# Keys and values built beside the last projection chunk; scores and retention products in array groups of their own

## The chip, the cores and the metric

One core of one Trainium2 chip runs the whole step as one launch. The time is device time in microseconds, the median of the runs shown below.

## The reference, cut to what matters

The program is one step of a decoder layer with a prompt of 1024 tokens and 8 decode sequences of 4 tokens each, on a past of 1024 tokens in pages.

```python
z = rms_norm(x, norm_mix) @ w_in               # q, three K/V pairs, retention q/k/v, gate columns
# attention group: 8 heads of 64, 2 K/V heads; three branches, gated sum
o_cmp = softmax(q kc) vc                       # 63 compressed blocks
o_sel = softmax(q k[selected blocks]) v        # here 16 blocks of 64 keys; decode leaves one of 17 out
o_win = softmax(q k[last 512]) v
# retention group: 4 heads, chunks of 128 tokens, state of 64 x 128 per head
s = (q k^T) * dec ; o = s v + (q state) * cross
state = g^128 * state + (k * w)^T v
h = x + [nsa ; retention] @ w_out
y = h + (silu(conv3(u W_u)) * (u W_v)) W_d     # u = rms_norm(h)
```

Everything is float32. Outputs are y, the new K/V rows, the window buffers, the retention states and the convolution states.

## The kernel before, in words

The program is written with a planner: pools hand out tiles, each instruction gets a place in a priority order (the order of the text, moved forward by a `high_priority` offset), and the planner fixes the order on each engine, the DMA issues of SyncE among them. At run time each engine works through its own list strictly; a DMA that waits for a buffer holds those queued behind it.

**Products.** A float32 product is two TensorE instructions. Large products use a high and a low part (`split`, lines 120 to 122: ScalarE copies the high part, VectorE or GpSimd subtracts) and add three products of the parts.

**Projections.** Nine token tiles (eight of 128 prompt tokens, the ninth 32 decode tokens) stand split in `XT[0..8]` (line 140). Six chunks of columns follow each other: `run(c, f, ...)` (line 925) takes chunk c through all tiles, in rising or falling order. Chunks 0 and 1 give the K/V rows, chunks 2 and 3 the retention, chunk 4 the queries, chunk 5 the retention gates (`ret_gate`, line 291, order 8 down to 0). Between tiles `run` advances a side generator by a number of steps: `compress_phase` in chunks 0 to 3, `decode_phase` in chunks 4 (2.5 steps a tile from the fourth on) and 5 (1 step a tile).

**Retention** (line 315). For each chunk and head `ob[h]` is the product of the decayed scores `at` with the values (128 rows, line 353) and, from the second chunk, of the queries `qc` with the state (64 rows, upper or lower half of the partitions by the head, line 355), added in the same place of PSUM. The banks alternate with the head. Line 341 makes the scores (64 rows), line 359 the new state (128 rows into 64 output partitions, upper or lower).

**Decode** (line 618). For each of four pairs B of sequences: `window_branch` and the steps of `compressed`, then `selected_branch`. `scores` (line 682) multiplies a tile of keys by `QB`: its columns 0 to 31 hold the queries of the first sequence, 96 to 127 those of the second, the rest zeros; each of the two products uses 64 columns, so that together they fill all 64 output rows of `XB`, the second added to the first. There is a `yield`, the end of a step, behind each product of keys. Keys come by page loads (`load_page`, line 451) of 128 KB into `GA[0]` and `GA[1]`; the window branch uses `GA[0]`, and pages of the selected branch are loaded there when it is done (line 809). Pages and windows pass through one SyncE queue.

**Keys and values.** `build(i)` (line 1259) loads 256 KB of finished K/V rows of a token tile from the output, splits the values into `VS` (ScalarE and GpSimd), transposes the keys on TensorE, and splits them into `KS` (ScalarE and VectorE). `KS` and `VS` lie in a pool of their own (line 992). The staging tile `STG` and the tile `FIN`, into which the masks are loaded first (line 1253), lie in the place of the first projection's tiles (`p1`, released in line 976). Builds 0 to 3 stand in front of the attention, 4 to 7 are the first four steps of `rest()`.

**Attention** (line 1103). For each token tile in the order 3, 2, 7, 6, 1, 0, 5, 4, for two K/V heads and two branches (selected with all earlier keys; window with the compressed keys): `softmax` (line 1032) makes the scores of four heads, `values_of` (line 1079) transposes the probabilities in blocks of 128 keys, splits them, and multiplies them by `VS`, or, for the last block of a window branch, which has 64 compressed keys, by `VC` (64 rows, lines 1092 and 1093). Each piece yields a cost; `beside(gen, ratio, cost)` (line 1238) advances the attention by ratio x cost for each step of another generator: first `rest()` (the builds and what is left of decode, 1.32), then the splitting of the output weights into `WO` (1.44 x 2.0), then the output projections of pairs of tiles (1.63, 18 steps each). The last output projection runs when the attention has ended, and `ffn_early` (line 1405) beside it.

**FFN.** Its seven operand tiles `X[1..7]` and later the tiles `h` lie in `p3h` (1, 2, 3), and in the places of `WO` (6, 7, 5, 4); four tiles of split weights lie in the place of `MIX`.

## Time and profile before

| what | value |
|---|---|
| median of 3 runs | 1564.74 us (1562.82 to 1569.26) |
| profiled execution | 1569.05 us |
| its span (first to last instruction) | 1567.3 us |
| TensorE busy | 1504.3 us, 96% |
| VectorE / ScalarE / GpSimd busy | 66% / 46% / 43% |
| mean granted TensorE clock | 0.98 |

The page gives one execution. The span is what its engines show; the execution's own time is 1.75 us longer. A busy share is a mean over stages that differ, so the rows further down are cut by stage. Starts are in us from the start of the span. The granted clock is given as a share of 2.4 GHz. Ends of TensorE instructions are modelled and overlap; the distance between starts tells how long one holds the engine.

### The profile page before, as it was taken

The page shows a single profiled execution, that of the slowest core. Times are in us where ns is not written, and L with a number is a line of the kernel's source. Part 1 is how long each engine was busy: PE and PEld are TensorE (multiplying, and loading weights), DVE is VectorE, ACT ScalarE, POOL GpSimd, SP SyncE. Part 2 cuts the span into 40 slices and gives each one's busy share as a digit, 9 for nine tenths or more (in the row PEclk, how much of TensorE's full clock was granted, in tenths as well). Part 3 has the DMA queues.
Part 4 walks back from the last instruction along what each step waited for, and adds up shares of the span by engine and source line. Part 5 has one row for each costly group of instructions (what it writes and reads, how often), then busy time and mean ns, then how long its engine had stood idle before and what let it go on. Part 6 is the DMA issues. An engine that isn't in the chain of part 4 may idle for free.

```text
span 1567.3 us, 28652 instructions
## 1 busy us (share of the span) xinstructions
PE 1504.3 (96%) x10338; PEld 1344.1 (86%) x10338; DVE 1038.6 (66%) x2023; ACT 717.2 (46%) x1564; POOL 679.5 (43%) x945
## 2 busy tenths in 40 slices
PE   7999999999899997999999899999999999999999
PEld 5898877766566665798988899999999999999999
DVE  7876523364388788766566987778878877644631
ACT  6454323233577667755555443333333334544431
POOL 3553211262366547656544143333333334444542
PEclk9999999999899999999999999999999999999999
DMA  8452300231412211001013224555554534887662
GB/s 269 147 153 68 87 11 27 58 124 57 161 60 68 84 41 54 28 15 45 28 29 95 73 89 144 163 172 173 168 171 164 169 135 148 287 258 214 208 197 66
DMA packets 126274, 184.43 MB, mean 118 GB/s; under 512 B 20388, under 2 KB 84772, under 8 KB 126132
## 3 DMA queue, kind: packets, MB, share of 16 engines
q1 hardware_dynamic: 124644, 177.97, 35.8%
q0 software_dynamic: 1488, 4.63, 0.9%
q8 instruction: 81, 1.33, 0.3%
q14 instruction: 61, 0.50, 0.1%
HBM read 132.73 MB, written 49.82 MB: 116 GB/s over the span
## 4 chain that ended last, share of the span: by engine, by line
PE 81%; DVE 8%; ACT 4%; issue 3%; DMA 3%; SPq 1%; POOL 0%; DVEq 0%; ACTq 0%; POOLq 0%
PE PS L459 49%; PE PS L230 5%; PE PS L233 5%; PE PS L232 5%; PE PS L1088 3%; PE PS L1204 2%; PE PS L1203 2%; PE PS L1205 2%; DVE live L1053 1%; PE PS L683 1%; DVE pt L122 1%; PE PS L353 1%; PE PS L355 1%; ACT pt L121 1%; ACT pwin L1054 1%
## 5 line engine op out<-in xcount | busy, mean ns | idle before, releaser
L459 PE MATMUL PS<-x,wop 128*128 128x264 f32 x3696 | 455.7, 286 | 9.0 <-ACT x L121 3.7
L459 PEld LDWEIGHTS PS<-x,wop 128*128 128x128 f32 x3696 | 453.6, 189 | 10.8 <-ACT x L121 4.1
L459 PE MATMUL PS<-h,wop 128*128 128x264 f32 x1848 | 225.7, 284 | 0.0
L459 PEld LDWEIGHTS PS<-h,wop 128*128 128x128 f32 x1848 | 225.5, 188 | 0.0
L122 POOL TENSOR_TENSOR wop<-st,wop 128x512 fp32r<-128x512 f32 (+1 forms) x105 | 139.3, 1333 | 177.3 <-ACT wop L121 173.7
L121 ACT ACTIVATE wop<-st 128x512 fp32r<-128x512 f32 x150 | 90.5, 608 | 205.6 <-PE PS L459 113.2
L230 PE MATMUL PS<-wh,xt 128*128 128x512 f32 (+1 forms) x432 | 168.9, 393 | 8.0 <-ACT xt L121 7.8
L233 PE MATMUL PS<-wh,xt 128*128 128x512 f32 (+1 forms) x384 | 148.5, 387 | 2.6 <-DVE xt L122 2.6
L232 PE MATMUL PS<-wl,xt 128*128 128x512 f32 (+1 forms) x384 | 148.5, 387 | 0.0
L122 DVE TENSOR_TENSOR pt<-PS,pt 128x512 fp32r<-128x512 f32 (+1 forms) x148 | 100.0, 684 | 40.7 <-ACT pt L121 24.8
L122 POOL TENSOR_TENSOR wop<-rawf,wop 128x512 fp32r<-128x512 f32 x42 | 70.7, 1684 | 119.8 <-ACT wop L121 119.8
L121 ACT ACTIVATE pt<-PS 128x512 fp32r<-128x512 f32 (+1 forms) x148 | 86.3, 596 | 57.9 <-PE PS L1088 29.2
L1053 DVE TENSOR_REDUCE live<-PS 128x1 f32<-128x640 f32 (+7 forms) x128 | 88.0, 701 | 32.7 <-PE PS L459 31.3
L230 PEld LDWEIGHTS PS<-wh,xt 128*128 128x128 f32 x432 | 83.8, 195 | 29.3 <-ACT xt L121 8.5
L459 PE MATMUL PS<-ks,qt 128*128 128x320 f32 (+5 forms) x400 | 102.2, 350 | 5.6 <-ACT psel L1054 4.1
L459 PE MATMUL PS<-pt,vs 128*128 128x512 f32 x264 | 103.1, 444 | 4.2 <-ACT pt L121 1.8
L233 PEld LDWEIGHTS PS<-wh,xt 128*128 128x128 f32 x384 | 74.6, 194 | 16.8 <-DVE xt L122 3.5
L232 PEld LDWEIGHTS PS<-wl,xt 128*128 128x128 f32 x384 | 74.6, 194 | 15.0 <-issue 2.6
L1077 POOL TENSOR_TENSOR pwin<-pwin,live 128x64 f32<-128x64 f32 (+5 forms) x128 | 80.2, 651 | 2.2
L1203 PE MATMUL PS<-mix,wo 128*128 128x256 f32 (+1 forms) x256 | 74.8, 293 | 2.3 <-ACT mix L121 2.3
L1072 POOL TENSOR_TENSOR live<-live 128x1 f32<-128x1 f32 (+1 forms) x128 | 24.7, 199 | 119.2 <-DVE live L1071 98.8
L459 PEld LDWEIGHTS PS<-ks,qt 128*128 128x128 f32 x400 | 64.8, 197 | 13.4 <-ACT psel L1054 5.6
(400 smaller groups left out, 2999.1 us busy)
## 6 DMA issues: line engine op xcount, KB each, us to landing
rawf<-in_w_ffn_in SPq DMA_DIRECT2D x30, 512.0 KB, 3.3
rawf<-scr_x SPq DMA_DIRECT2D x51, 264.0 KB, 3.7
scr_x<-rbig SPq DMA_DIRECT2D x44, 264.0 KB, 2.6
ws<-in_w_ffn_out SPq DMA_DIRECT2D x64, 176.0 KB, 3.0
scr_s<-ws SPq DMA_DIRECT2D x64, 176.0 KB, 2.4
scr_x<-qbig SPq DMA_DIRECT2D x33, 264.0 KB, 2.1
raw<-in_w_in SPq DMA_DIRECT2D x17, 512.0 KB, 3.6
ga<-in_cache_sel SPq DMA_DIRECT2D x64, 128.0 KB, 2.0
```

The costliest lines, as they stand in the source:

```text
L121: a = S.activation(h, src, AF.Copy)
L122: return a.ins, (eng or V).tensor_tensor(l, src, b32(h), ALU.subtract).ins
L230: T.matmul(ps, xh(i, kk), wh[:, k], start=first, stop=False)
L232: T.matmul(ps, xh(i, kk), wl[:, k], start=False, stop=False)
L233: T.matmul(ps, xl(i, kk), wh[:, k], start=False, stop=end)
L459: T.matmul(o, a, b, start=start, stop=stop, skip_group_check=True)
L1053: V.tensor_reduce(nm[:, r:r + 1], src, AX.XY, ALU.max, negate=True)
L1077: G.tensor_tensor(a, a, f.to_broadcast([128, a.shape[1]]), ALU.mult)
L1088: T.transpose(tb[:, r * 128:(r + 1) * 128], pp[r][:, c:c + n], ident)
L1203: T.matmul(o, wh, MIX[:, 0, k, 0:n], start=k == 0, stop=False)
L1204: T.matmul(o, wh, MIX[:, 1, k, 0:n], start=False, stop=False)
L1205: T.matmul(o, wl, MIX[:, 0, k, 0:n], start=False, stop=k == 7)
```

## The change

- Token tiles 4 to 7 move to a pool `pa`, two to a tile (`a0`: 7 and 6, `a1`: 5 and 4). This pool stays to the end: behind the fifth tile of chunk 5 (order 8, 7, 6, 5, 4) its two places become `KS` and `VS`, and in the FFN the tiles 1 and 2.
- `building` takes the place of `plain` in chunk 5: behind the tiles 3, 2, 1, 0 it calls `build(0)` to `build(3)`, whose rows are staged in `HN` and in the place of `XT[8]`. Builds 4 to 7 stay in `rest()`.
- Retention: the four products with `at` come first, the four with the state behind them; only the first product in each bank has `start`.
- Decode: `QB` has 64 columns; each sequence's product uses 32 columns and writes 32 output rows of its own. In `window_branch` and `selected_branch` there is one `yield` for two products, and the next queries are made at z == 3 where it was z == 5.
- `VC` gets its upper 64 rows as a copy of the lower ones; the two halves of the split probabilities stand above each other, and one product of 128 rows takes the place of two. Its cost for the pacing is 0.6 where it was 0.85.
- FFN: `SLOT` gives the places of the tiles; 1 and 2 lie in `pa`, 4 in the place of `MIX`, and the four weight tiles in the place of `wo3`.

```diff
--- before
+++ after
@@ -127,6 +127,7 @@
 
 
     NW = 5
+    pa_ = open_pool("pa", "right")
     p1 = open_pool("p1", "right")
     ICT = mk(p1, "ict", IC.size)
 
@@ -137,7 +138,10 @@
     HN = mk(p1, "hn", 528)
     SQ = HN[:, 0:256]
     ones = live("ones")
-    XT = [mk(p1, f"xt{i}", 2048, F32R) for i in range(8)] + [mk(p1, "xt8", 576, F32R)]
+    XA_ = [pa_.tile([128, 8 * HALF], F32R, name=f"xa{z}", tag=f"a{z}") for z in range(2)]
+    XT = [mk(p1, f"xt{i}", 2048, F32R) for i in range(4)]
+    XT += [XA_[(7 - i) // 2][:, (7 - i) % 2 * 2048:(7 - i) % 2 * 2048 + 2048] for i in range(4, 8)]
+    XT += [p1.tile([128, 576], F32R, name="xt8", tag="xt8")]
     WH, WL = [[mk(p1, f"{x}{i}", 1024, F32R) for i in range(NW)] for x in ("wh", "wl")]
     RAW = [mk(p1, f"raw{i}", 1024) for i in range(2)]
     tables = {}
@@ -350,9 +354,10 @@
             st = STATE.rearrange("p (a e) -> p a e", e=128)
             for h in range(4):
                 a, p = h // 2, (h % 2) * 64
-                T.matmul(ob[h], at[:, h], hv[h], start=True, stop=i == 0)
-                if i:
-                    T.matmul(ob[h], qc[p:p + 64, a], st[p:p + 64, a], start=False, stop=True)
+                mm(ob[h], at[:, h], hv[h], start=h < 2, stop=i == 0)
+            for h in range(4 if i else 0):
+                a, p = h // 2, (h % 2) * 64
+                mm(ob[h], qc[p:p + 64, a], st[p:p + 64, a], stop=True)
             ub = PS[:, 3, 0:256].rearrange("p (a e) -> p a e", e=128)
             for h in range(4):
                 a, p = h // 2, (h % 2) * 64
@@ -582,6 +587,7 @@
                 for g in range(2):
                     T.matmul(o[:, g], wg[:, g], w2[:, 128:192], start=True, stop=True)
                 split(VC[0:64, :, 0:64], VC[0:64, :, 64:128], o)
+                S.activation(VC[64:128], b32(VC[0:64]), AF.Copy)
 
         src = O["kv"][0:1024, 0:256].rearrange("(c s) (e d) -> c s e d", s=16, d=64)
 
@@ -619,7 +625,7 @@
         pd = open_pool("pd", "left")
         GA = [mk(pd, f"ga{i}", 2048) for i in range(2)]
         VP = [mk(pd, f"vp{i}", 512, F32R) for i in range(2)]
-        QB = mk(pd, "qb", 192)
+        QB = mk(pd, "qb", 64)
         KCB = mk(pd, "kcb", 128)
         P = mk(pd, "pdp", 1024)
         PD = mk(pd, "ptd", 1280, F32R).rearrange("p (j b h c) -> p j b h c", b=2, h=2, c=32)
@@ -679,8 +685,8 @@
         V.memset(b32(PD[:, 9]), 0.0)
         yield
 
-        def scores(out, k, b, last=1):
-            T.matmul(out, QB[:, b * 64:b * 64 + 64], k, start=b != last, stop=b == last)
+        def scores(out, k, b):
+            T.matmul(out[b * 32:b * 32 + 32], QB[:, b * 32:b * 32 + 32], k, start=True, stop=True)
 
         def queries(B):
             tb = t_bank()[:, 0:128].rearrange("p (a c) -> p a c", a=4)
@@ -689,7 +695,7 @@
             for h in range(8):
                 a, p, g = h // 2, (h % 2) * 64, (h // 4) * 64
                 src = tb[p:p + 64, a, B * 8:B * 8 + 8].rearrange("p (b t) -> p b t", t=4)
-                dst = QB[g:g + 64].rearrange("p (b c) -> p b c", c=96)[:, :, h:h + 32:8][:, :, 0:4]
+                dst = QB[g:g + 64].rearrange("p (b c) -> p b c", c=32)[:, :, h:32:8]
                 if h % 2:
                     V.tensor_copy(dst, src)
                 else:
@@ -752,9 +758,9 @@
             for a in (P[:64, 0:n], pn):
                 V.tensor_scalar(a, a, r, None, ALU.mult)
 
-        def key_scores(src, b, last=1):
-
-            scores(XB[:64], src.rearrange("p (j c) -> p j c", c=256)[:, :, 0:128], b, last)
+        def key_scores(src, b):
+
+            scores(XB[:64], src.rearrange("p (j c) -> p j c", c=256)[:, :, 0:128], b)
 
         def transposed(n):
             for hf in range(n // 4):
@@ -795,7 +801,7 @@
         def window_branch(B):
             for b in range(2):
                 key_scores(GA[0][:, b * 1024:(b + 1) * 1024], b)
-                yield
+            yield
             new_keys(B, 1, 1)
             V.tensor_tensor(XB[:64, 0:4], XB[:64, 0:4], dc("winm"), ALU.add)
             V.tensor_reduce(NM[:, 0:1], XB[:64], AX.X, ALU.max, negate=True)
@@ -815,8 +821,8 @@
                 load_page()
             for hf in range(2):
                 for b in (1, 0):
-                    key_scores(GA[b][:, hf * 1024:(hf + 1) * 1024], b, 0)
-                    yield
+                    key_scores(GA[b][:, hf * 1024:(hf + 1) * 1024], b)
+                yield
                 po = P[:64, hf * 512:(hf + 1) * 512]
                 pv, xv = [t.rearrange("p (b e) -> p b e", e=64) for t in (po, XB[:64])]
                 V.tensor_tensor(pv, xv, dn[:, hf * 8:hf * 8 + 8].unsqueeze(2).to_broadcast([64, 8, 64]), ALU.add)
@@ -872,7 +878,7 @@
             for _ in other:
                 yield
             for z, _ in enumerate(selected_branch(B)):
-                if z == 5 and B < 3:
+                if z == 3 and B < 3:
                     yield from queries(B + 1)
                 yield
         tb = t_bank()[:, 0:128].rearrange("p (k c) -> p k c", c=32)
@@ -972,7 +978,37 @@
     side = decode_phase()
     next(side)
     run(4, q_proj, staged, down, side, SB[0], 3)
-    run(5, ret_gate, plain, down, side, SB[1])
+    kv_ = {}
+
+    def build(i, z):
+
+        D.dma_start(z, O["kv"][i * 128:(i + 1) * 128, 256:768])
+        zb = z.rearrange("p (b c) -> p b c", c=256)
+        v = zb[:, :, 128:256].rearrange("p b (g d) -> p b g d", d=64)
+        split(kv_["v"][:, i, :, :, 0:64], kv_["v"][:, i, :, :, 64:128], v, G)
+        tb = t_bank()[:, 0:256].rearrange("p (b t) -> p b t", b=2)
+        for b in range(2):
+            T.transpose(tb[:, b], zb[:, b, 0:128], ident)
+        tk = slice(i * 128, (i + 1) * 128)
+        for g in range(2):
+            kh, kl = kv_["k"][0:64, :, g, tk], kv_["k"][64:128, :, g, tk]
+            S.activation(kh, tb[g * 64:(g + 1) * 64], AF.Copy)
+            V.tensor_tensor(kl, tb[g * 64:(g + 1) * 64], b32(kh), ALU.subtract)
+
+    def building(f, order):
+
+        for z, i in enumerate(order):
+            f(i, i == order[-1])
+            if z == 4:
+                k, v = [pa_.tile([128, 8 * HALF], F32R, name=n, tag=t)[:, 0:4096] for n, t in (("ks", "a0"), ("vs", "a1"))]
+                kv_["k"] = k.rearrange("p (b g t) -> p b g t", b=2, g=2)
+                kv_["v"] = v.rearrange("p (i b g c) -> p i b g c", i=8, b=2, g=2)
+                st = [HN[:, 0:512], p1.tile([128, 576], F32, name="st8", tag="xt8")[:, 0:512]]
+            elif z > 4:
+                build(z - 5, st[z % 2])
+            yield
+
+    run(5, ret_gate, building, down, side, SB[1])
     p1.release()
 
 
@@ -989,10 +1025,7 @@
     PSEL = [mk(p2, f"psel{i}", 1024) for i in range(4)]
     PT = [mk(p2, f"pt{i}", 1024, F32R) for i in range(RPT)]
     PWIN = [mk(p2, f"pwin{i}", 704) for i in range(4)]
-    pkv = open_pool("pkv", "right")
-    KSt, VSt = mk(pkv, "ks", 4096, F32R), mk(pkv, "vs", 4096, F32R)
-    KS = KSt.rearrange("p (b g t) -> p b g t", b=2, g=2)
-    VS = VSt.rearrange("p (i b g c) -> p i b g c", i=8, b=2, g=2)
+    KS, VS = kv_["k"], kv_["v"]
     OT = PS[:, 6]
     del ring[:]
 
@@ -1081,17 +1114,22 @@
         pp = (PSEL, PWIN)[br]
         jobs = [(b * 128, 128, VS[:, w0 // 128 + b, br, g]) for b in range(nw // 128)]
         if br:
-            jobs.append((640, 64, VC[0:64, g]))
+            jobs.append((640, 64, VC[:, g]))
         for z, (c, n, vv) in enumerate(jobs):
             tb = t_bank()[0:n]
             for r in range(4):
                 T.transpose(tb[:, r * 128:(r + 1) * 128], pp[r][:, c:c + n], ident)
-            pt = PT[ctr["pt"] % RPT][0:n]
+            pt = PT[ctr["pt"] % RPT]
             ctr["pt"] += 1
-            split(pt[:, 0:512], pt[:, 512:1024], tb)
-            mm(OT, vv, pt[:, 0:512], start=br == 0 and z == 0)
-            mm(OT, vv, pt[:, 512:1024], stop=br == 1 and z == len(jobs) - 1)
-            yield 0.85
+            if n == 64:
+                split(pt[0:64, 0:512], pt[64:128, 0:512], tb)
+                mm(OT, vv, pt[:, 0:512], stop=True)
+                yield 0.6
+            else:
+                split(pt[:, 0:512], pt[:, 512:1024], tb)
+                mm(OT, vv, pt[:, 0:512], start=br == 0 and z == 0)
+                mm(OT, vv, pt[:, 512:1024])
+                yield 0.85
         if br:
             S.activation(FIN[0:64], OT[64:128], AF.Copy)
             f = q_ap(i)[:, g * 256:(g + 1) * 256].rearrange("p (k t) -> p k t", t=128)
@@ -1256,25 +1294,9 @@
     V.tensor_copy(m192[:, 0:128], mc("mdiag"))
     V.tensor_copy(cmpm, mc("cmpm"))
 
-    def build(i):
-
-        z = STG[:, i % 4 * 512:i % 4 * 512 + 512]
-        D.dma_start(z, O["kv"][i * 128:(i + 1) * 128, 256:768])
-        zb = z.rearrange("p (b c) -> p b c", c=256)
-        v = zb[:, :, 128:256].rearrange("p b (g d) -> p b g d", d=64)
-        split(VS[:, i, :, :, 0:64], VS[:, i, :, :, 64:128], v, G)
-        tb = t_bank()[:, 0:256].rearrange("p (b t) -> p b t", b=2)
-        for b in range(2):
-            T.transpose(tb[:, b], zb[:, b, 0:128], ident)
-        tk = slice(i * 128, (i + 1) * 128)
-        for g in range(2):
-            kh, kl = KS[0:64, :, g, tk], KS[64:128, :, g, tk]
-            S.activation(kh, tb[g * 64:(g + 1) * 64], AF.Copy)
-            V.tensor_tensor(kl, tb[g * 64:(g + 1) * 64], b32(kh), ALU.subtract)
-
     def rest():
         for i in range(4, 8):
-            build(i)
+            build(i, STG[:, i % 4 * 512:i % 4 * 512 + 512])
             yield
         while True:
             with tc.high_priority(offset=QP):
@@ -1282,11 +1304,9 @@
                     return
             yield
 
-    for i in range(4):
-        build(i)
     beside(rest(), R[0], 1.0)
     pw_ = open_pool("pwo", "left")
-    WO = [pw_.tile([128, 8 * HALF], F32R, name=f"wo{q}", tag=f"wo{q}")[:, 0:4096].rearrange(
+    WO = [pw_.tile([128, 8 * HALF if q < 3 else 4096], F32R, name=f"wo{q}", tag=f"wo{q}")[:, 0:4096].rearrange(
         "p (h k c) -> p h k c", h=2, k=8) for q in range(4)]
     beside(load_w(), R[2], 2.0)
     MIX = pm.tile([128, 4608], F32R, name="mix", tag="mix").rearrange("p (h k t) -> p h k t", h=2, t=288)
@@ -1402,10 +1422,17 @@
         elif p == 3:
             load_raw(f + 1, 1)
 
+    SLOT = {1: (pa_, "a0"), 2: (pa_, "a1"), 6: (pw_, "wo0"), 7: (pw_, "wo1"), 5: (pw_, "wo2"), 4: (pm, "mix")}
+
+    def slot_tile(p, name):
+
+        pool, tag = SLOT[p]
+        return pool.tile([128, 4608 if p == 4 else 8 * HALF], F32R, name=name, tag=tag)[:, 0:8 * HALF]
+
     def ffn_early():
 
         for p in (1, 2, 3):
-            X[p] = x_tile(p3h.tile([128, 8 * HALF], F32R, name=f"x{p}", tag=f"x{p}"))
+            X[p] = x_tile(slot_tile(p, f"x{p}"))
         RAWF.extend(mk(p3h, f"rawf{z}", 1024) for z in range(2))
         RAWF.append(QBIG[:, 4096:5120])
         WOP.extend(mk(p3h, f"wop{z}", 1024, F32R) for z in range(3))
...
@@ -1442,8 +1469,8 @@
             yield
 
     def ffn():
-        X[4] = x_tile(pw_.tile([128, 8 * HALF], F32R, name="x4", tag="wo3"))
-        wm = pm.tile([128, 4608], F32R, name="wop", tag="mix")
+        X[4] = x_tile(slot_tile(4, "x4"))
+        wm = pw_.tile([128, 4096], F32R, name="wop", tag="wo3")
         WOP.extend(wm[:, z * 1024:(z + 1) * 1024] for z in range(4))
         prep(3)
         d = inverse_rms(2, PS[:, 5])
...
@@ -1653,9 +1677,9 @@
         if todo:
             last = not main_alive and seen == NT
             if last:
-                pkv.release()
                 p2.release()
                 p3h = open_pool("p3h", "right")
+                SLOT[3] = p3h, "x3"
                 early = ffn_early()
                 ffn_t["m"] = 0
             a = todo.pop(0)
...
```

## Rows read from the trace of the kernel before

**Rows 1.** The page, parts 1 and 4: busy time of engines with their share of the span, and the chain that ended last by engine.

```profile
PE 1504.3 (96%) x10338; PEld 1344.1 (86%) x10338; DVE 1038.6 (66%) x2023; ACT 717.2 (46%) x1564; POOL 679.5 (43%) x945
...
PE 81%; DVE 8%; ACT 4%; issue 3%; DMA 3%; SPq 1%; POOL 0%; DVEq 0%; ACTq 0%; POOLq 0%
```

**Rows 2.** Busy time by stage: the stretch in us, its length, busy us (instructions) of TensorE, of its weight loads, of VectorE, ScalarE and GpSimd, then the granted TensorE clock as a share of full speed, the DMA share and GB/s.

```profile
205.00:295.00 90.00, 90.00 (x492) 66.99 (x491) 35.08 (x104) 26.77 (x95) 16.20 (x18) 0.98 0.13 37
345.00:412.00 67.00, 64.50 (x284) 46.57 (x282) 28.48 (x88) 24.31 (x52) 19.11 (x21) 0.95 0.23 74
412.00:447.00 35.00, 25.48 (x112) 17.91 (x111) 24.33 (x73) 24.18 (x69) 18.74 (x32) 0.76 0.46 149
447.00:612.00 165.00, 152.51 (x859) 110.46 (x859) 132.25 (x339) 112.98 (x314) 99.33 (x161) 0.97 0.18 56
635.00:847.00 212.00, 205.70 (x1472) 185.55 (x1469) 137.55 (x333) 123.45 (x332) 113.56 (x223) 1.00 0.11 32
```

**Rows 3.** TensorE in order of time in the retention stage. Columns: start us, us from the first start to the last end, engine, line, operation, out<-in, shape, count. The start of the next row tells when the engine went on.

```profile
209.87 1.06 PE L353 MATMUL PS<-tt,tt 128*128 128x128 f32 x8
210.76 0.27 PE L324 MATMUL PS<-pers,qbig 128*128 128x128 f32 x1
...
227.00 0.66 PE L359 MATMUL PS<-tt,tt 128*64 128x128 f32 x8
227.59 0.72 PE L341 MATMUL PS<-tt 64*128 64x128 f32 x8
228.24 0.49 PE L353 MATMUL PS<-tt,tt 128*128 128x128 f32 x2
228.66 0.48 PE L355 MATMUL PS<-state,tt 64*128 64x128 f32 x2
...
231.57 0.50 PE L230 MATMUL PS<-wh,xt 128*128 128x512 f32 x1
```

**Rows 4.** TensorE in order of time at a pair of score products and what follows it; then the weight loads of the same line grouped (busy us, mean ns).

```profile
576.52 1.93 PE L683 MATMUL PS<-ga,qb 128*64 128x512 f32 x4
578.38 0.73 PE L459 MATMUL PS<-pt,vs 128*128 128x512 f32 x2
...
L683 PEld LDWEIGHTS PS<-ga,qb 128*64 128x64 f32 x48 | 5.5, 136 | 11.7 <-issue 10.6 <-DVE qbig L811 0.4 <-DVE qbig L261 0.4
```

**Rows 5.** TensorE in order of time beside the attention: one 64-row product with VC and its follower, and three 128-row products with VS and their follower.

```profile
525.95 0.50 PE L459 MATMUL PS<-pt,vc 64*128 64x512 f32 x1
526.38 0.42 PE L683 MATMUL PS<-kn,qb 128*64 128x32 f32 x4
...
559.93 0.94 PE L459 MATMUL PS<-pt,vs 128*128 128x512 f32 x3
560.71 0.22 PE L459 MATMUL PS<-mo_r,idr 128*128 128x128 f32 x1
```

**Rows 6.** TensorE in order of time from the last projection product to the first scores of the attention.

```profile
411.04 0.39 PE L233 MATMUL PS<-wh,xt 128*128 128x512 f32 x1
...
425.03 0.69 PE L1268 MATMUL PS<-pers,stg 128*128 128x128 f32 x2 [1.93 <-DMA stg<-out_kv]
425.37 2.48 PE L459 MATMUL PS<-ks,qt 128*128 128x512 f32 x6
```

**Rows 7.** What TensorE waited for (engine, line, waited for, us in total, times, longest): from 447 to 612 us the first row, and from 412 to 872 us the one of line 683.

```profile
PE PS L459 <- ACT psel L1054: 1.6, 4, 0.8
...
PE PS L683 <- issue: 2.6, 1, 2.6
```

**Rows 8.** The chain that ended last, between 395 and 450 us (start us, us, what): the mask load's issue and the two waves of loads of finished tokens.

```profile
412.87 0.36 SPq L75
...
414.24 4.57 DMA stg<-out_kv
...
419.70 5.29 DMA stg<-out_kv
```

**Rows 9.** VectorE in order of time: the last of the mask copies before the first score.

```profile
415.97 0.18 DVE L1111 CAST m<-cmpm 128x64 fp32r<-128x64 f32 x1
```

**Rows 10.** Groups of instructions over the whole run (busy us, mean ns): two pieces of a build.

```profile
L1273 DVE TENSOR_TENSOR ks<-PS,ks 64x256 fp32r<-64x256 f32 x16 | 6.7, 422 | 4.1 <-ACT ks L1272 3.7
...
L122 POOL TENSOR_TENSOR vs<-stg,vs 128x256 fp32r<-128x256 f32 x8 | 5.7, 727 | 8.2 <-ACT vs L121 8.1
```

**Rows 11.** The DMA queue of SyncE: eight page loads in order of time, and the queue's longest wait from 340 to 430 us.

```profile
402.78 9.98 SPq L456 DMA_DIRECT2D ga<-in_cache_sel  x8
...
SPq L662 <- POOL vp L122: 22.3, 1, 22.3
```

**Rows 12.** TensorE in order of time at the end of the attention and the start of the last output projection.

```profile
844.49 0.73 PE L459 MATMUL PS<-pt,vc 64*128 64x512 f32 x2
847.50 0.50 PE L1203 MATMUL PS<-mix,wo 128*128 128x256 f32 x2 [2.29 <-ACT mix L121]
```

**Rows 13.** What TensorE waited for from 860 to 910 us, the first row.

```profile
PE PS L459 <- ACT x L121: 3.7, 2, 1.9
```

8 lines of the change are left out of this document (3 added, 5 removed).

## Prediction

> **What bounds the kernel now.** I read the page's busy shares and chain first: TensorE is busy 96% of the span and makes up 81% of the chain that ended last, VectorE and ScalarE lie at 66% and 46% [rows 1]. So I looked at TensorE stage by stage [rows 2]. From 205 to 295 us (retention) it is busy without a break, the others under 40%: each product saved is time. From 345 to 412 us (last two projection chunks, decode beside them) it is nearly the same. From 412 to 447 us it is busy 25.48 of 35 us, at a granted clock of 0.76: this stretch is bound by something else. From 447 to 612 (decode beside attention) and 635 to 847 us (output projection beside attention) it is busy 92% and 97%. The FFN behind that keeps its instructions; only its tiles change places.
>
> The timelines then show three kinds of waste and a hole. In the retention, products on 128 and on 64 rows alternate, two instructions each: from 228.24 to 231.57 us eight pairs take 3.33 us, 0.416 a pair [rows 3]. The same 128-row products in one run took 0.89 us for eight instructions (209.87 to 210.76), 0.111 each. So of 0.416 some 0.2 is the change of shape. The score products (four instructions a pair of sequences) hold TensorE 1.86 us [rows 4]. The 64-row product with VC takes 0.43 us, where a 128-row one with the same 512 columns takes 0.26 in a run (0.78 for three) [rows 5]. The hole: the last projection instruction starts at 411.04, so it ends near 411.3; the first score of the attention starts at 425.37 [rows 6].
>
> **Retention, lines 351 to 355.** The four 128-row products come first, the four 64-row ones behind, on alternating row halves and banks. Chunk 0 shows the first run: 0.89 us. Line 341 has the form of the second (64 rows, 128 columns, alternating halves): 0.65 us for eight, the change behind it included [rows 3]. So 3.33 - 0.89 - 0.65 = 1.79 us a chunk, seven chunks: 12.5 us. If the halves did not overlap, eight would take 8 x 0.111 + 0.2 = 1.09 and the saving is 9.5; the other end is 13. I take 12.5, as line 341's row has the very form. Chunk 0 and the decode chunk keep theirs.
>
> **Scores, line 683.** 64 zero-padded columns and an accumulation become two 32-column products into different output partitions, and the yield between them goes. Without the shape change of 0.2 an instruction costs (1.86 - 0.2) / 4 = 0.415 us. Line 359 shows two column groups beside each other: eight instructions in 0.59 us, (0.59 - 0.2) / 8 = 0.05 each where 0.111 is the single one, so they overlap fully [rows 3]. A pair then costs 2 x 0.415 + 0.2 = 1.03 us, 0.83 less. There are 12 pairs: 10.0 us. No row has 32 columns at this length; the ends are 0 (no overlap) and 10.0, and I take line 359's. Three pairs (first two sequences) lie in the full projection stretch: 2.5 us. Nine lie beside the attention: 7.5 us, of which I count 0.85, because TensorE is idle there 3 to 8% of the time and a shorter queue meets more of the waits on ScalarE and VectorE that stand there now [rows 2, 7]: 6.3. Together 8.8.
>
> The Trainium skill ("TensorE: Matmul & The Clock Gate", Part 3, The mechanism) says that weight loads overlap running products only when the row groups differ; a score pair differs in column groups alone. By it two of a pair's four loads, 0.136 us each [rows 4], would stand bare, and the saving would be 12 x 0.27 = 3.3 us smaller. The column-group row above speaks against that.
>
> **Values of the compressed keys, line 1093.** Hi and lo halves of p are stacked, so two 64-row products become one of 128 rows: 2 x 0.43 - 0.26 = 0.60 us [rows 5], 16 times: 9.6; times 0.85: 8.2 us (ends 4.8 and 9.6). The product now waits for VectorE's half too; other blocks' products stand between, as for all other blocks. The one added copy on ScalarE costs nothing: it runs while the projections hold TensorE.
>
> **Keys and values built earlier, lines 1259 to 1286.** Today the staging tile lies in the place of the finished tokens, so four 256 KB loads can start only after the last projection. The chain runs through two waves of them, 4.57 and 5.29 us, and a transpose of build 4 at 425.03 stands in TensorE's queue ahead of the first score [rows 6, 8]. Afterwards builds 0 to 3 are done by then. What is late next is the masks: their load was issued at 412.87, and the last mask copy ran at 415.97 [rows 8, 9]. So the first score can start near 416.2, 4.9 us after the projections instead of 14.1: 9.2 us. Against it stand eight transposes at 0.111 us that now lie in the full projection stretch: 0.9. A build's three VectorE and GpSimd pieces (0.42, 0.42, 0.73 us) [rows 10] lie beside engines busy 28 and 19 of 67 us [rows 2]; without that cover four builds cost 6 us. Their four loads go into SP's queue. There a window load waited 22.3 us for a buffer that GpSimd reads, and eight page loads took 9.98 us to issue [rows 11]; a build's load behind such a wait is late, the ScalarE copy that waits for it blocks the next gate activation, and this blocks the bank of the next projection but one. Ends: 0, and 12 us if the masks come early too. I take 8.3.
>
> **Pacing.** By the yields in the code, decode has 90 steps before and 78 after. The projections take 25, so 65 become 53 beside the attention. The three or four further steps done in the projections (a score pair and the small products of the second window, some 2 us) filled the hole until now; now they cost: -2. With four builds, 69 steps x 1.32 = 91 units of attention pass before the output weights are split; afterwards 57 x 1.32 = 75. Weights add 23, three output projections 88. Attention has 194 units (190 afterwards, 16 x 0.25 less). Before, it ended 8 units ahead of the third output projection; in the trace it ends at 844.49 just as this is through [rows 12]. Afterwards it ends some 4 units behind, alone, where each block waits for its own ScalarE and VectorE halves: -3 us (ends 0 and -6).
>
> **New places in the FFN.** Tile x4 takes MIX's place and four weight tiles take wo3's; the last product of the output projection frees both, so nothing moves. The first splits there cost 3.7 us of waiting today [rows 13]; I allow 2 us either way and count 0.
>
> **Sum.** 12.5 + 8.8 + 8.2 + 8.3 - 2 - 3 = 32.8 us. The profiled execution took 1569.05 us (span 1567.3 and 1.75 around it), so it would be 1536.3. It is the slowest but one reading here: the median of the timed runs is 1564.74. From this the forecast is 1532.
>
> **Rivals.**
> A, the builds come late: a load is caught in SP's queue as told above, and the hole stays. For it speaks that 22.3 us wait; against it that the planner orders SP by the time at which a load is ready. Gain 32.8 - 8.3 = 24.5: 1540.
> B, what is saved beside the attention does not come through, because ScalarE, VectorE and GpSimd chains set its pace. For it: VectorE is busy 132 of 165 us there [rows 2]. Against: all listed waits of TensorE on others from 447 to 612 us are short, the largest 1.6 us in four [rows 7]. It loses 6.3 + 8.2: gain 18.3, 1546.
> C, slower: page waits. Without the yield, a sequence's second score of a selected half stands right behind the first, while its eight page loads have just been queued; they need 9.98 us to issue and about 2 to land. If the order on TensorE puts it there, everything queued behind (scores, values, projections) waits up to 12 us, four times: 48 us lost, 15 slower than before, 1580. It decides from 33 us, 8 us for each of four rounds. Against it: TensorE's longest wait at this line today is 2.6 us [rows 7], and the planner can still put work between.
> D, the two loads of a pair's second product stand bare: 3.3 us less, 1535. Line 359's eight instructions in 0.59 us speak against it [rows 3].
> That packing is undone (other work put between the two products of a pair) is part of B and D.
>
> **How the numbers follow.** Forecast 0.64, A 0.13, B 0.13, D 0.04, C 0.06. Low end: 12.5 + 10.0 + 9.6 + 12 - 2 = 42 us and a little for waits that shrink at full clock: 1520. High end: 9.5 for the retention, no overlap of scores, half of the values (4.8), half of the hole (4.6), -5 for pacing give 14 us: 1551; the range 1519 to 1552 leaves out C and the two tails. About 0.5% (8 us) can be told from no change. Faster by more: forecast, A, D and nearly all of B, 0.90; within: some of B and half of C's mild forms, 0.05; slower 0.05.
>
> **What would show it.** Retention: runs of eight instructions of line 353's and 355's kind at 0.89 and 0.65 us; if the second takes 1.09, the halves do not overlap. Scores: 1.03 us a pair; 1.86 means no overlap. VC products in 128-row form at 0.26 us. First score of the attention some 5 us after the last projection instruction, at about 400 us into the run. The 910 to 1567 us stretch as long as before. Wrong if TensorE waits at line 683 for tens of us (C), if the first score still comes 14 us late (A), or if idle shares beside the attention grow by what the products shrink (B).

## The result, and the profile after

The changed kernel takes 1555.7 us (median of 12 runs, 1552.65 to 1560.8) beside 1567.86 us for the kernel before (12 runs, 1562.3 to 1573.7): ratio 0.9925, 95% interval 0.9906 to 0.9945, some 12 us. I had forecast 33. The page's first part and the stages answer to [rows 1, 2]:

```profile
span 1551.5 us, 28635 instructions
...
PE 1478.1 (95%) x10322; PEld 1332.1 (86%) x10322; DVE 1033.4 (67%) x2023; ACT 717.7 (46%) x1565; POOL 682.4 (44%) x945
```

Stages, columns as in [rows 2]:

```profile
205.00:295.00 90.00, 90.00 (x580) 69.43 (x578) 38.06 (x112) 27.75 (x96) 20.37 (x21) 1.00 0.13 38
335.00:400.00 65.00, 59.43 (x277) 43.41 (x275) 29.16 (x96) 26.07 (x57) 17.94 (x20) 0.95 0.29 90
400.00:417.00 17.00, 8.97 (x37) 4.62 (x35) 10.01 (x31) 10.35 (x29) 5.84 (x9) 0.74 0.34 101
435.00:600.00 165.00, 143.33 (x802) 107.71 (x801) 129.63 (x324) 113.29 (x304) 105.69 (x159) 0.89 0.19 59
602.00:832.00 230.00, 220.27 (x1594) 200.91 (x1592) 159.35 (x375) 139.99 (x369) 130.57 (x248) 1.00 0.13 37
```

TensorE is busy for 26 us less and is no better used: beside the decode (435 to 600) it is busy 143 us in place of 152.5, at a clock of 0.89 in place of 0.97. The products themselves shrank as forecast. TensorE in order of time, a chunk of the retention [rows 3], two score pairs [rows 4] and a product with VC [rows 5]:

```profile
225.12 1.16 PE L464 MATMUL PS<-tt,tt 128*128 128x128 f32 x8
226.21 0.71 PE L464 MATMUL PS<-state,tt 64*128 64x128 f32 x8
226.85 0.50 PE L234 MATMUL PS<-wh,xa 128*128 128x512 f32 x1
...
357.75 1.05 PE L689 MATMUL PS<-ga,qb 128*32 128x512 f32 x4
358.73 0.50 PE L236 MATMUL PS<-wl,xa 128*128 128x512 f32 x1
...
402.41 1.05 PE L689 MATMUL PS<-ga,qb 128*32 128x512 f32 x4 [0.60 <-issue]
403.50 0.34 PE L860 MATMUL PS<-pers,qbig 64*128 64x64 f32 x2
...
520.48 0.40 PE L464 MATMUL PS<-pt,vc 128*128 128x512 f32 x1
520.72 0.25 PE L464 MATMUL PS<-m,idr 128*128 128x192 f32 x1
```

From start to start: 1.73 us a chunk (3.33 before; the other six chunks take 1.63 or 1.64), 0.98 a pair of sequences (1.86), 1.09 for the pair behind a wait, 0.24 for the VC block (two of 0.43). But the hole behind the projections, [rows 6], grew from 14.3 to 17.3 us. TensorE from the last projection instruction to the first score:

```profile
399.29 0.39 PE L237 MATMUL PS<-wh,xt 128*128 128x512 f32 x1
...
404.57 0.44 PE L991 MATMUL PS<-pers,hn 128*128 128x128 f32 x2 [0.74 <-DVE dsm L752]
409.05 0.69 PE L769 MATMUL PS<-pers,pdp 64*128 64x64 f32 x4 [4.05 <-DVE pdp L759]
409.67 0.69 PE L991 MATMUL PS<-pers,st 128*128 128x128 f32 x2
...
412.34 0.69 PE L991 MATMUL PS<-pers,hn 128*128 128x128 f32 x2
...
416.36 0.44 PE L464 MATMUL PS<-m,idr 128*128 128x128 f32 x1 [1.64 <-DVE cmpm L1295]
416.60 1.17 PE L464 MATMUL PS<-ks,qt 128*128 128x512 f32 x2
```

The transposes of three of the four builds (line 991) still stand here, among waits for the decode's probabilities (dsm and pdp, lines 752 to 759), and the masks are last. The DMA queue of SyncE:

```profile
355.68 0.34 SPq L985 DMA_DIRECT2D hn<-out_kv  x1
...
389.04 15.94 SPq L461 DMA_DIRECT2D ga<-in_cache_sel  x10
405.08 0.37 SPq L985 DMA_DIRECT2D hn<-out_kv  x1
406.28 6.96 SPq L461 DMA_DIRECT2D ga<-in_cache_sel  x3
413.29 0.43 SPq L75 DMA_DIRECT2D fin<-in_const  x1
```

The first load into hn (build 1) was issued at 355.68; its transposes ran at 404.57, long after it can have landed (the loads into hn take 3.0 us in the median), and only then the next load into hn (build 3) was issued, at 405.08. The masks' load left 14.0 us behind the last projection instruction, where it was 1.8 before (412.87 behind 411.04). At the far end the third output projection is through at 804.7 and the attention goes on alone, up to its last product at 831.9 [rows 12]. Two windows of 29 us:

```profile
775.00:804.00 29.00, 29.00 (x227) 27.86 (x227) 15.82 (x31) 14.70 (x36) 13.96 (x24) 1.00 0.06 19
805.00:834.00 29.00, 24.38 (x150) 19.16 (x148) 23.30 (x49) 18.17 (x42) 14.03 (x22) 1.00 0.29 92
```

Of the second window's 4.6 us without work, 2 lie behind the attention, in the wait for mix that the kernel before has too (2.29 us in [rows 12]); the rest are the attention's own.

The books from the first score to the last VC product, cut into windows of 5 us (idle is length less busy; half clock is busy times one less the granted clock; work is the rest): before 419.2 us = 380.9 work + 25.7 idle + 12.6 half clock; after 415.5 = 361.9 + 34.2 + 19.4. So 19.0 us of work went, and 15.3 came back as waiting and slow clock.

One run below, h5, has its trace from a slow execution alone, at a granted clock of 0.741, so no times of that trace are given.

### The profile page after: what moved, and what is told of

It is laid out like the page before. It is cut to its first block, busy times and chain, and to the rows that moved or that the text cites. A ratio compares the mean times of both kernels' runs of the same rounds, so it can differ in the third digit from the quotient of the medians.

```text
span 1551.5 us, 28635 instructions
## 1 busy us (share of the span) xinstructions
PE 1478.1 (95%) x10322; PEld 1332.1 (86%) x10322; DVE 1033.4 (67%) x2023; ACT 717.7 (46%) x1565; POOL 682.4 (44%) x945
## 4 chain that ended last, share of the span: by engine, by line
PE 82%; DVE 8%; ACT 3%; issue 3%; DMA 2%; POOL 1%; SPq 1%; DVEq 0%; ACTq 0%; POOLq 0%
PE PS L464 53%; PE PS L234 5%; PE PS L237 5%; PE PS L236 5%; PE PS L1121 3%; PE PS L1241 2%; PE PS L1242 2%; PE PS L1243 2%; DVE live L1086 1%; DVE pt L122 1%; ACT pt L121 1%; PE PS L689 1%; PE PS L791 1%; DMA pers<-in_const 1%; ACT pwin L1087 0%
## 5 line engine op out<-in xcount | busy, mean ns | idle before, releaser
L122 DVE TENSOR_TENSOR pt<-PS,pt 128x512 fp32r<-128x512 f32 (+1 forms) x148 | 100.4, 684 | 27.9 <-ACT pt L121 17.3
L464 PE MATMUL PS<-ks,qt 128*128 128x320 f32 (+5 forms) x400 | 105.4, 357 | 5.5 <-ACT psel L1087 2.4
L234 PE MATMUL PS<-wh,xt 128*128 128x512 f32 (+1 forms) x240 | 94.7, 396 | 7.4 <-ACT xt L121 6.9
L1241 PE MATMUL PS<-mix,wo 128*128 128x256 f32 (+1 forms) x256 | 75.1, 294 | 3.1 <-ACT mix L121 2.3
L237 PE MATMUL PS<-wh,xt 128*128 128x512 f32 (+1 forms) x192 | 75.4, 394 | 2.6 <-DVE xt L122 2.6
L236 PE MATMUL PS<-wl,xt 128*128 128x512 f32 (+1 forms) x192 | 75.0, 391 | 0.0
L1110 POOL TENSOR_TENSOR psel<-psel,live 128x512 f32<-128x512 f32 (+7 forms) x64 | 73.7, 1156 | 2.9
L234 PE MATMUL PS<-wh,xa 128*128 128x512 f32 (+1 forms) x192 | 74.0, 386 | 0.9 <-DVE hn L245 0.7
L1242 PE MATMUL PS<-mix,wo 128*128 128x256 f32 (+1 forms) x256 | 74.6, 292 | 0.1
```

The lines of the kernel that those rows point to most:

```text
L122: return a.ins, (eng or V).tensor_tensor(l, src, b32(h), ALU.subtract).ins
L234: T.matmul(ps, xh(i, kk), wh[:, k], start=first, stop=False)
L236: T.matmul(ps, xh(i, kk), wl[:, k], start=False, stop=False)
L237: T.matmul(ps, xl(i, kk), wh[:, k], start=False, stop=end)
L464: T.matmul(o, a, b, start=start, stop=stop, skip_group_check=True)
L1110: G.tensor_tensor(a, a, f.to_broadcast([128, a.shape[1]]), ALU.mult)
```

## The experiments

All runs but h5 in one table: ratio to the kernel before on the same chip with its 95% interval; start of the last projection instruction; time from there to the first score; from the first score to the start of the last products with VC; start of the last output-projection product. The last column is worked out from the code: units of attention that the yields drive (steps beside it times the ratio, plus 23 and 88) less the units it has (194, with the VC edit 190).

| kernel | ratio | last projection | hole | attention | out-projection ends | units over |
|---|---|---|---|---|---|---|
| before | 1 | 411.0 | 14.3 | 419.1 | 873.0 | +8 |
| changed | 0.9925 (0.9906 to 0.9945) | 399.3 | 17.3 | 415.3 | 861.0 | -4 |
| s1 retention alone | 0.9996 (0.9976 to 1.0016) | 398.5 | 12.4 | 423.8 | 864.0 | +8 |
| s2 VC alone | 1.0027 (1.0012 to 1.0042) | 409.3 | 14.1 | 421.1 | 875.3 | +12 |
| s3 scores alone | 1.0111 (1.009 to 1.0133) | 406.5 | 19.9 | 430.7 | 886.2 | -8 |
| s4 builds alone | 0.9987 (0.9972 to 1.0003) | 414.0 | 10.1 | 419.2 | 870.8 | +8 |
| s5 scores, old steps | 0.9957 (0.9941 to 0.9974) | 406.6 | 11.8 | 418.0 | 866.8 | +8 |
| u1 changed, retention undone | 1.0041 (1.0023 to 1.0059) | 409.0 | 17.3 | 421.8 | 877.5 | -4 |
| u2 changed, VC undone | 1.0043 (1.0027 to 1.0059) | 401.8 | 17.5 | 434.3 | 884.3 | -8 |
| u3 changed, scores undone | 0.9996 (0.9984 to 1.0009) | 401.8 | 9.8 | 419.7 | 871.2 | +12 |
| h1 loads by GpSimd | 0.9953 (0.9933 to 0.9972) | 401.3 | 20.3 | 414.7 | 865.9 | -4 |
| h2 masks by GpSimd | 0.9924 (0.9907 to 0.9941) | 398.6 | 19.9 | 411.6 | 860.0 | -4 |
| p1 ratio 1.6 | 0.9923 (0.9902 to 0.9943) | 400.3 | 17.3 | 410.8 | 860.9 | +12 |
| c1 h1 and p1 | 0.9932 (0.9917 to 0.9947) | 401.1 | 19.9 | 409.5 | 860.0 | +12 |
| h4 builds cut loose | 0.9886 (0.9858 to 0.9915) | 397.5 | 4.6 | 423.3 | 855.6 | -4 |
| v1 changed, old steps | 0.9908 (0.9883 to 0.9934) | 396.6 | 8.4 | 421.8 | 857.2 | +12 |
| b1 h4 and v1 | 0.9872 (0.985 to 0.9894) | 398.7 | 3.4 | 419.9 | 850.8 | +12 |
| b2 b1, ratio 1.4 | 0.9935 (0.9914 to 0.9957) | 398.8 | 3.4 | 422.4 | 863.4 | +18 |
| n1 before, ratio 1.09 | 1.0154 (1.0126 to 1.0181) | 410.9 | 12.8 | 440.7 | 893.3 | -8 |

**One part alone.** Each is the kernel before with one piece of the diff shown above: line 353 ff. (s1), the VC copy and block (s2), `scores`, `QB` and the yields (s3), `building` and the tile places (s4).

> The kernel before with the retention products regrouped, and nothing else. Theory 'places' (the retention and projection terms came out as forecast, the terms at the start of the attention and beside it were lost): 12 us faster, ratio about 0.992, which is the whole gain of the change. Rival 'everything shrinks' (each term is worth about a third of its forecast): 4 to 5 us faster. In the trace both expect 1.09 + 0.64 us for the two runs of a chunk.

> The kernel before with the values of the compressed keys as one 128-row product, and nothing else. Theory 'engines set the pace beside the attention' (my rival B): 0 to 3 us faster. Theory 'only the pacing of the whole change lost it': alone, with the old pacing in which the output projection ends the stage and the attention never stands alone, the forecast 8 us come through.

> The kernel before with the decode scores as two 32-column products, the yields between them gone, and nothing else. Theory 'engines set the pace beside the attention': 2.5 us from the three pairs in the projections and at most 2 us more, so 2 to 4 us faster. Theory 'lost by pacing or by the blocked load queue of the moved builds': 6 to 9 us faster.

> The kernel before with the first four key and value builds moved beside the last projection chunk (and the new places of the tiles), and nothing else. Theory 'caught in the load queue': the first score of the attention still comes 14 us or more after the last projection, and the time is the same or up to 4 us slower. Theory 'only in the company of the shorter decode': the page loads come at another time here, the first score comes about 5 us after the last projection, 5 to 8 us faster.

No part alone is faster by more than 0.2%, and the scores are 17 us slower. In s1 the projections end 12.5 us early and the output projection 9 us; the span gains 3.9 us, the median nothing. So 'places' held up to 864 us and failed behind it. s2 has, in books as above, 8.3 us less TensorE work than the kernel before and 10.0 us more of idle time and half clock: the saving came back as waiting, as 'engines set the pace' says, and the kernel is even some 4 us slower, where that theory had 0 to 3 faster. s3 was outside both theories. s4 fits neither as a whole: the hole shrank to 10.1 us, not to 5, while the projections took 2.9 longer, and the time is the same.

**The hole: load queue or something else?** h1 issues the loads of builds 0 to 3 and of the masks from GpSimd, h2 the masks' alone:

```diff
-        D.dma_start(z, O["kv"][i * 128:(i + 1) * 128, 256:768])
+        G.dma_start(z, O["kv"][i * 128:(i + 1) * 128, 256:768])
...
-    section("MC", FIN[:, 0:MC.size])
+    section("MC", FIN[:, 0:MC.size], G)
```

> The changed kernel with the loads of builds 0 to 3 and of the masks issued from GpSimd's queue in place of SyncE's. Theory 'blocked load queue makes the hole' : the first score comes 4 to 8 us after the last projection (17 now), and the time falls by 8 to 11 us. Rival 'the hole comes from the end of the last projection chunk itself (activations and VectorE copies into places that come free late)': the loads land early, the first score still comes 12 us or more late, gain under 4 us. Second rival 'the gain is given back behind': the hole shrinks, and the end of the attention moves by less than half of that.

> The changed kernel with only the load of the masks issued from GpSimd's queue; the builds stay on SyncE's. If the masks alone hold the first score: 17 us shrink to about 5 and the time falls as in the run with both. If builds 0 to 3 hold it too (the fourth build's load was issued at 405 us): the first score waits for the last build's keys and comes about 14 us late, gain 2 to 3 us.

The hole stayed, 20.3 and 19.9 us. GpSimd's queue in h1:

```profile
407.32 0.56 POOL L985 DMA_DIRECT2D hn<-out_kv  x1 [2.26 <-PE PS L991]
...
414.17 1.42 POOL L122 TENSOR_TENSOR vp<-ga,vp 128x256 fp32r<-128x256 f32 x2 [2.33 <-ACT vp L121]
415.53 0.56 POOL L75 DMA_DIRECT2D fin<-in_const  x1
```

The second load waits for the transposes that free its staging place, not for a queue; and the masks' load is caught behind the decode's work on GpSimd as it was on SyncE. So h1 takes the load queue out as the cause for the builds and says nothing on the masks, and neither does h2, where GpSimd issues their load at 412.81.

The transposes in turn take a PSUM bank from the ring of three that the decode uses, whose steps run late by the length of their chains; that was my next theory. h4 gives builds 0 to 3 banks 4 and 5 (free in this chunk), four staging places (the raw weight tiles, free by then), and them and the masks the decode's priority; h5 changes the bank alone:

```diff
-        tb = t_bank()[:, 0:256].rearrange("p (b t) -> p b t", b=2)
+        tb = (PS[:, 4 + i % 2] if i < 4 else t_bank())[:, 0:256].rearrange("p (b t) -> p b t", b=2)
...
+            if z == 0:
+                st = [RAW[j // 2][:, j % 2 * 512:j % 2 * 512 + 512] for j in range(4)]
+                for j in range(4):
+                    D.dma_start(st[j], O["kv"][j * 128:(j + 1) * 128, 256:768])
...
+                with tc.high_priority(offset=SP):
+                    build(z - 5, st[z - 5])
```

> The changed kernel with builds 0 to 3 cut loose from the decode: four staging places of their own, loaded at the start of the last chunk; PSUM banks 4 and 5 in place of the ring of three that the decode uses; the masks' load and copies, and the builds, at the decode's priority. Theory 'ring of banks' (a build's transposes wait for the bank that a late decode step still holds): the four builds' transposes stand before 390 us, the first score comes 5 to 8 us after the last projection in place of 17, and the time falls by 8 to 11 us against the changed kernel. Rival 'the decode's own chain makes the hole': builds early, but TensorE still waits about 4 us for the decode's probabilities ahead of the first score; 12 us or more, gain 0 to 4 us.

> The changed kernel with only the PSUM bank of builds 0 to 3 changed (4 and 5 in place of the ring). Theory 'ring of banks': builds 0 and 1 before 390 us, but the masks' load (413.3 us) now holds the first score at about 416, so the hole stays at 15 us or more and the time within 3 us of the changed kernel. If the masks were never last: the hole falls below 10 us here already.

h5 came out at 0.9907 (0.9878 to 0.9936), which can be told neither from the changed kernel nor from h4; what the bank does alone stays open. In h4 the builds' transposes lie at 345 to 367 us, and TensorE goes on at once:

```profile
366.95 0.60 PE L992 MATMUL PS<-pers,raw 128*128 128x128 f32 x4
...
397.51 0.39 PE L237 MATMUL PS<-wh,xt 128*128 128x512 f32 x1
...
401.96 0.33 PE L464 MATMUL PS<-m,idr 128*128 128x128 f32 x1 [0.28 <-DVE m L1299]
402.12 0.44 PE L464 MATMUL PS<-ks,qt 128*128 128x512 f32 x1
```

With banks, staging and priority changed together, the masks' included, the hole is closed (4.6 us); which of them does most is open, and the steps of the next section shorten it too. Of its 12.7 us (and 1.8 at the projections) only 5.4 arrive at the end of the output projection: the attention takes 8.0 us longer. The gain in time, some 6 us on the changed kernel, is less than the 8 to 11 expected, and the two intervals touch.

**The pacing.** p1 raises the ratio, c1 adds h1 to it, v1 and s5 give the decode its old number of steps back, the pair still together:

```diff
-    R = (1.32, 1.06, 1.44, 1.63)
+    R = (1.6, 1.06, 1.44, 1.63)
```

```diff
             for b in range(2):
                 key_scores(GA[0][:, b * 1024:(b + 1) * 1024], b)
             yield
+            yield
```

> The changed kernel with the pacing ratio of the decode stage at 1.6 in place of 1.32, so that the shorter decode (57 steps) carries 91 units of attention again and not 75. Theory 'pacing': the attention no longer stands alone at the end (815 to 835 us) and the gap behind the decode (575 to 595 us) closes; 4 to 8 us faster. Theory 'engines set the pace': within 2 us of the changed kernel.

> Both: loads of the first builds and masks from GpSimd's queue, and the ratio at 1.6. If the hole and the pacing are two separate causes, the gains of the two single runs add: 12 to 19 us faster than the changed kernel. If the saving at the hole only makes the attention end earlier than the output projection, the sum is no more than the larger of the two.

> The changed kernel with a second yield behind each score pair, so that the decode has as many steps as before, the pair still together. Theory 'fewer steps push the decode's chains into the last projections and starve the rest': TensorE's stall in the projections (2.9 us at 341.7) and the hole shrink, decode beside the attention is stretched, 5 to 9 us faster than the changed kernel. Theory 'engines set the pace': the idle time moves, within 2 us.

> The kernel before with the scores in two column groups, but with as many steps as before (two yields behind each pair). Against the run of scores alone, which was 1.1% slower. Theory 'the lost yields made it slower': here 4 to 9 us faster than before, 20 us and more faster than the run without the yields. Theory 'column groups themselves cost' : still 10 us or more slower than before.

s5 settles the scores: 0.4% faster, where without the steps they are 1.1% slower; the column groups pay and the lost yields cost 24 us there. In the changed kernel the same steps (v1) or the ratio (p1, and with h1's loads c1) are worth nothing that the ratios show, though v1 ends the output projection 3.8 us earlier. p1 does not: its attention ends 3.6 us earlier and its output projection where it was.

For the hole the steps decide more than the loads. With the builds moved and the old number of steps it is 8.4 to 10.1 us (v1, u3, s4); with the builds moved and fewer steps 17.3 to 20.3 (the changed kernel, u1, u2, h1, h2, p1, c1); with fewer steps and the builds in their old place 19.9 (s3), where s5 has 11.8. Among the kernels with fewer steps h4 alone has it closed. The 25 steps that the projections take carry the decode further when a step holds more; the probabilities of lines 752 to 759 then stand between the last projection and the builds. In v1 they do not. Its DMA queue, and TensorE behind the last projection instruction (396.60):

```profile
386.84 0.37 SPq L987 DMA_DIRECT2D hn<-out_kv  x1
388.34 9.76 SPq L461 DMA_DIRECT2D ga<-in_cache_sel  x8
398.21 0.37 SPq L75 DMA_DIRECT2D fin<-in_const  x1
...
396.83 0.38 PE L993 MATMUL PS<-pers,hn 128*128 128x128 f32 x2
...
401.69 0.69 PE L993 MATMUL PS<-pers,stg 128*128 128x128 f32 x2 [2.56 <-DMA stg<-out_kv]
```

The last load into hn leaves 18 us earlier than in the changed kernel, the masks' load 1.6 us behind the projections, and what holds the first score now is build 4's rows (stg), which are loaded behind the masks. Here too the attention takes longer (6.5 us).

n1 changes the pacing of the kernel before, and no work:

> The kernel before with nothing but the pacing ratio of the decode stage at 1.09 in place of 1.32: its 69 steps then carry 75 units of attention, as the 57 steps of the run of scores alone do, and no work is removed. Theory 'too little attention beside the decode, the attention ends alone': its end comes 8 to 13 us later, as in the scores run (844.5 to 857.1 us), and the kernel is 8 to 17 us slower. Rival 'the score run lost its time at the decode's chains, not at the pacing': within 4 us of the kernel before.

22 us slower, more than expected and nearly as much as the lost yields cost in s3 (24 us), so the pacing alone can account for most of that. Its end, in two windows, with the attention alone in the second:

```profile
800.00:833.00 33.00, 32.11 (x243) 30.20 (x242) 18.65 (x39) 17.41 (x41) 18.03 (x27) 1.00 0.05 17
833.00:867.00 34.00, 26.61 (x153) 20.66 (x151) 23.28 (x50) 18.63 (x43) 12.97 (x21) 0.90 0.26 78
```

The three kernels 8 units short (s3, u2, n1) need 431 to 441 us for the attention, all others 410 to 424. The last are spread without an order: 4 short or 8 to 12 over makes no clear difference.

**One part undone in the changed kernel.**

> The changed kernel with the retention products as before, all else kept. Alone the retention edit gave nothing (ratio 0.9996), though its profile had the last projection 12.5 us and the last output projection 9 us earlier. Theory 'work removed from a TensorE-bound stretch counts, the rest is the order of what follows': undoing it costs 9 to 13 us here. Theory 'given back whatever follows': within 3 us of the changed kernel.

> The changed kernel with the two 64-row products for the values of the compressed keys as before. Alone the edit removed 9.1 us of TensorE work and added 9.7 us of idle time. Theory 'beside the attention TensorE is no longer the bound': undoing it costs nothing (within 3 us of the changed kernel, or faster). Rival 'its saving counts in this company': 6 to 9 us slower.

> The changed kernel with the score products and their yields as before. Alone, scores with fewer yields were 17 us slower, with as many steps 7 us faster. Theory 'the lost steps cost what the column groups save': within 4 us of the changed kernel. Rival 'in this company the column groups count': 6 to 9 us slower.

Undone, each part costs 11 to 18 us, more than either theory had, and alone, with the yields as the change has them, each gave nothing. For VC the table has a reason: its block drives the pacing with 0.6 in place of 0.85, and without that the attention is 8 units short. That fits; it was not run by itself. For the retention, 9.7 of the 16.5 us stand at the last projection already. For the scores the trace of u3 has the whole loss behind the attention: that ends at 831.3, in the changed kernel at 831.9, but the last output projection takes 39.9 us from there in place of 29.1, with 8.8 us of TensorE idle in place of 2.4. The longest wait there is ahead of a product of the FFN's norm:

```profile
847.33 1.01 PE L1341 MATMUL PS<-live,qbig 128*128 128x1 f32 x4 [5.65 <-POOL qbig L1201]
```

So u3's 11 us are no price of the score products.

**Both remedies.**

> The changed kernel with the builds' own banks, staging and priority and with the decode's old number of steps. If the two gains are separate they add: some 6 us and 3 us, ratio about 0.985. If both shorten the same hole: no better than the builds' banks alone (0.9886).

> The run with own banks and the old number of steps (ratio 0.987), with the pacing ratio at 1.4 in place of 1.32, so that the 65 steps carry the 91 units of before. If the pacing still costs something: 2 to 5 us faster. If it is even: within 2 us. A change of over 4 us to the slower side would show that a neutral shift of the order alone moves the time by that much.

b1 is the fastest here: 1547.5 us, 20 us under the kernel before. The two remedies come to 0.39% and 0.17% singly and 0.53% together; that agrees with a sum, but the 0.17% alone is inside the intervals. In b2's expectation I miscounted: the steps beside the attention are 69, so b1 already has the 91 units and b2 drives 97. It is some 9 us slower, with no instruction added or removed; in its trace the first FFN products stand inside the last output projection and wait there for their operands (1.92 us for x at 835.86), as in u3. So a shift of the order alone is worth some 9 us here, and one kernel's difference of that size is no price of the part that was edited.

## Why the prediction was wrong

By stage, against the kernel before: the projections end 11.8 us earlier, the hole takes 3.0 of that back, the attention gives 3.8, the last output projection takes 0.6. That is the 12.0 us by which the output projection ends earlier. The forecast had 12.1, 9.2 and 11.5 for the first three.

- **Prices of the products: right.** Retention 1.60 to 1.70 us a chunk (forecast 1.79), a score pair 0.88 (0.83), VC 0.62 (0.60). The last projection instruction came 11.75 us earlier; my terms say 12.1 (12.5 and 2.5, less 0.9 and 2). Alone, the retention gave its 12.5, but the scores 4.6 where I had 0.5 and the builds cost 2.9 where I had 0.9, so part of the match is luck. Rivals C and D fell: TensorE's longest wait ahead of a pair on loaded pages is 0.60 us, and four loads and products take 0.98 us, where D needs 1.30.
- **"So the first score can start near 416.2, 4.9 us after the projections instead of 14.1": the step that failed most.** It started there, at 416.6, but the projections were through 12 us sooner: the hole is 3.0 us longer where I had counted 9.2 less. I took builds 0 to 3 as done because their loads would be early. Three of the four loads were; but the transposes of three builds stood behind the projections, among the waits for the decode's probabilities, and the fourth load waited for a staging place. Two prices were too low. The lost yields, for which I had -2, put those probabilities there: with the old steps the hole is 8.4 us (v1). And build 4's rows and transposes, which I had seen ahead of the first score before the change [rows 6], stay there: s4 moves only the builds and has 10.1 us, not 4.9. Rival A had the effect, not the cause: build 1's rows lay ready for some 45 us. The "what is late next" was the masks, as I said. h4 moves masks and builds together, so it doesn't show what each holds alone.
- **"Of which I count 0.85": the other step that failed.** Of 14.5 us for scores and VC beside the attention, 3 of pacing taken off, 11.5 should have shown between the first score and the last VC product; 3.8 did. That is mostly rival B, which I gave 0.13. I judged by the length of the waits of before, the largest 1.6 us in four [rows 7]. The waits grew as TensorE's queue got shorter. TensorE's waits (us in total, times, longest) from 425 to 845 us before, two rows, and from 416 to 832 us after the change, longest in total; the last two rows are s2 from 423 to 845 us:

```profile
PE PS L459 <- ACT psel L1054: 5.3, 8, 1.6
...
PE PS L459 <- DVE pt L122: 1.4, 2, 0.7
...
PE PS L464 <- DVE pt L122: 7.7, 12, 3.1
PE PS L1121 <- ACT pwin L1087: 3.3, 4, 1.1
PE PS L464 <- ACT pt L121: 3.1, 7, 0.8
PE PS L464 <- ACT psel L1087: 2.6, 2, 2.4
...
PE PS L459 <- DVE pt L122: 8.1, 10, 2.5
PE PS L459 <- ACT pt L121: 6.7, 7, 3.0
```

  What grew most is the wait for the low parts of the probabilities, which VectorE subtracts (pt, line 122). s2, where only VC is changed, has it too, and waits longer for the high parts from ScalarE besides (6.7 us, 1.8 before). So the chain that makes the probabilities set the pace there. In b1, with the hole closed and the pacing whole, the same stretch has 14.9 us less work than before and 15.9 more of idle and half clock (9.6 and 6.3): all of it given back. Some 3.7 us of work that stood in the hole before is inside that stretch now, so the products themselves saved that much more than 14.9.
- **"Pacing: -3": not shown as a price.** The attention alone at the end idles some 3 us (4.6 of 29, less the wait for mix), which is the size. But p1, where TensorE is busy without a break from 800 to 829 us, gains nothing, and v1's 3.8 us come with a shorter hole. Four units further, n1's output projection ends 20 us later: I had no such cliff in the sum.
- **FFN: nothing moved.** From the last output-projection product to the end 690.5 us after 694.3. Between the kernels this stretch lies between 690 and 699 with the same products; s1 has the 699, with TensorE waiting 3.8 us in six for VectorE's sums from 940 to 1400 us where before had 1.7 in two. Why the whole 9 us of s1 are gone in its median stays open.

## What to carry to other kernels

Where TensorE was busy 92% beside three engines that feed it, most of what was saved came back as waiting: count a saved product there at nothing until a run shows otherwise. Where the others were under half busy the saving came through to the end of the stage (12.5 us in s1), though even this was gone at the end of s1's run. When a step is moved earlier, follow every resource that it shares with late work (PSUM bank, staging place, in-order queue), not its load alone, and what else the change puts in front of it. And when the number of yields or their costs changes, work the pacing out anew: the same instructions differed by 22 us.

## What was not expected of the hardware

A wait can cost more than its length. TensorE in windows of 5 us in the changed kernel, columns as above:

```profile
469.00:474.00 5.00, 4.24 (x27) 2.79 (x27) 4.94 (x18) 3.25 (x11) 1.11 (x3) 1.00 0.10 26
474.00:479.00 5.00, 2.95 (x21) 2.13 (x19) 4.70 (x20) 4.70 (x18) 4.42 (x12) 1.00 0.29 79
479.00:484.00 5.00, 4.80 (x20) 3.31 (x19) 3.71 (x10) 1.42 (x5) 1.91 (x4) 0.59 0.00 0
484.00:489.00 5.00, 5.00 (x26) 4.35 (x26) 3.16 (x10) 1.90 (x6) 1.42 (x2) 0.73 0.00 2
```

TensorE idles 2.05 us from 474 to 479, and then works at a granted clock of 0.59 and 0.73, that is partly at 1.2 GHz in place of 2.4: 4.80 x 0.41 + 5.00 x 0.27 = 3.3 us more. Not every wait does this at once: in the window from 805 to 834 us above TensorE idles 4.6 us in all at a granted clock of 1.00, and only the stretch behind it, 834.7 to 861.0, has 0.94. Which waits bring the clock down is not shown by these runs.
